# Reciprocals of the softmax sums by way of DRAM rows instead of a spread, a transpose and a copy

## Chip, cores and metric

One core of one Trainium2 chip. The metric is the device time of one execution in microseconds, the median of the runs. Engines are named as in the profile: PE is TensorE, DVE is VectorE, ACT is ScalarE, POOL is GpSimd, SP is the engine that here only issues DMAs.

## What is computed

One layer of a diffusion transformer trunk in float32: adaLN-modulated norms around a mixing layer (pooling in one half of the width, 2-D neighbourhood attention in the other) and a squared-ReLU MLP. SEQ = 1024 latent tokens on a grid of 16 rows by 64 columns, 256 context tokens, 8 heads of 64. The change touches the attention alone:

```python
s_loc = jnp.einsum('bnqhd,brnkhd->bhnqrk', q_r, k_b).astype(jnp.float32) * scale
...
s_loc = jnp.where(col_mask, s_loc + bias.astype(jnp.float32), -jnp.inf)
s_ctx = jnp.einsum('bnqhd,bkhd->bhnqk', q_r, k_ctx).astype(jnp.float32) * scale
...
s = jnp.concatenate([s_loc.reshape(B, H, NA_NCB, NA_QB, n_loc), s_ctx], axis=-1)
p = jax.nn.softmax(s, axis=-1).astype(v.dtype)
...
o = (jnp.einsum('bhnqrk,brnkhd->bnqhd', p_loc, v_b)
     + jnp.einsum('bhnqk,bkhd->bnqhd', p_ctx, v_ctx))
```

## The kernel before

The attention is cut into 32 units. Unit i has a pair of heads, `j = i // 8` (e = 0, 1 in the code), and a band of 8 grid columns, `m = i % 8`, which is 128 queries. Its keys are the bands m-1, m, m+1 (128 each) and the 256 context tokens: 640, or 512 in the bands at the edges (m = 0 and 7), which here are called edge units.

Queries stand on partitions in the scores and in the probabilities. For the product with the values, keys have to stand on partitions, so PE turns the probabilities by transposes in 64-row halves. The result of the value products, `pa`, has the head's channels on partitions and the 128 queries along the free axis. The softmax is divided only there: by then the reciprocal of each query's sum is needed in another layout, constant over the 64 partitions of a head and running over queries along the free axis.

One Python loop of N + 4 = 36 passes writes the work out, shifted: in pass i, `weighed(i - 4)`, then `scores(i)` (PE, then DVE adds bias and mask with a running minimum, `nm`, line 998), `turn(i - 2)` and `fifth_kept(i - 2)`, the exponentials `exps(i, ...)` on ACT, `turn_kept(i - 2, ...)`, `share(i - 1)` and `values(i - 3)`. The order on PE, ACT, DVE and SP is the order of the loop (`in_order`); each engine waits by semaphores only.

The names that matter:

- `share` (1009): DVE takes the reciprocal `ri` (128 x 2) of the two sums, and spreads it to `rb`, 128 x 128 (`tensor_copy`, 1013).
- `turn` (1018): PE transposes, first the two halves of `rb`, then in inner units the fifth block of the probabilities, into `sides`, which are columns of the PSUM banks `pa` and `pz`; then the other blocks into the banks `T` (1026).
- `fifth_kept` (1036): ACT copies the sides to SBUF, `px` (1040): 192 columns each in inner units, 64 in edge units.
- `turn_kept` (1042): ACT and DVE copy the two `T` banks to `pt`.
- `values` (1048): PE adds the value products up in `pa` (1060), 128 of its columns for even units and 128 for odd ones.
- `weighed` (1065): DVE multiplies `pa` by the turned share in `px` and writes the heads' page `f` (1070).

The units' loop also holds the loads of the output weights and their splitting. On SP's queue stand, in the order of the loop: the table loads `U` (876) in passes 2, 10 and 18; `accsh` in pass 4; `ss` in passes 5 and 6; `wor` (1102) in passes 8, 16, 26 and 28; `Ga` in pass 30; six loads `to1`, `bo22`, `to3` of the output weights (1143) in pass 32, 512 KB each. POOL builds the bias tables (883) and issues accumulating DMAs (188), among them two in pass 32 that add a second weight block to `to1`. From pass 32 on the first output products (`pox`) run on PE between the last units: x[0] in pass 32 to x[3] in pass 35. After the loop, PE goes on with `pox`, `poz` and `poy`, then with the MLP.

Of the kernel before, what the change touches and what calls it, by code (L numbers as in the profile page):

```python
# [11 lines left out]
F32 = mybir.dt.float32  # L12
# [6 lines left out]
P = 128  # L19
# [7 lines left out]
HD = 64  # L27
# [8 lines left out]
NM = GW // QC  # L36
# [44 lines left out]
def hybrid_block(ctx, tc, x, ctx_in, w_mod, b_mod, gp1, gp2, w_in, pool_w, rpb, w_out, w1, w2, vectors,  # L81
                 mask, edge, out):
    nc = tc.nc
    sub, mul, add = ALU.subtract, ALU.mult, ALU.add
# [6 lines left out]
    dram = ctx.enter_context(tc.tile_pool(name="dram", bufs=1, space=DRAM))  # L91
# [4 lines left out]
    def sm(name, n, bufs=1):  # L96
        return small.tile([P, n], F32, tag=name.split("_")[0], name=name, bufs=bufs)
# [173 lines left out]
    with tc.tile_pool(name="ps1", bufs=6, space=PSUM) as ps1, tc.tile_pool(name="tmp1", bufs=3) as tmp:  # L271
# [53 lines left out]
        inverse = {}  # L325
# [235 lines left out]
        for k in range(KT):  # L561
            for i in range(2):
                o = (k % 2) * 256 + i * P
# [235 lines left out]
        def row_sum(i):  # L799
            name, _, k = rows[i]  # L800
            if name not in accs:
# [5 lines left out]
        turns = {"w": iter([(pair_load, pair_split, i) for i in range(len(pairs))]),  # L807
                 "r": iter([(row_load, row_sum, i) for i in range(len(rows))])}
# [122 lines left out]
        with in_order(ET.PE, ET.Pool, ET.Activation, ET.DVE, ET.SP) as pooling:  # L931
            banks = {of: [bank(f"p{of}{j}") for j in range(2)] for of in "KQ"}
            use(-1)
            for step, (n, of, j) in enumerate([(n, of, j) for n, of in products for j in range(2)]):
                half_product(n, of, j, banks[of])
                use(step)
                if step in (5, 9, 17):
                    name = {5: "S1", 9: "S4", 17: "S3"}[step]
# [4 lines left out]
                if step in (7, 11):  # L943
                    name = {7: "S4", 11: "S3"}[step]
# [11 lines left out]
    with (  # L956
# [52 lines left out]
        def share(i):  # L1009
            ri = sm(f"ri_{i}", 2, 2)  # L1010
            nc.vector.reciprocal(ri, sums[i])
            shares[i] = att.tile([P, P], F32, tag="ri", name=f"rb{i}", bufs=2)
            nc.vector.tensor_copy(shares[i].rearrange("p (e t) -> p e t", e=2),
                                  ri.rearrange("p (e o) -> p e o", o=1).to_broadcast([P, 2, HD]))

        def turn(i):
            inner = 0 < units[i][1] < NM - 1
            t = [bank(f"T{i}_{h}") for h in range(2)]  # L1020
            turned[i] = t
            halves = [slice(h * HD, (h + 1) * HD) for h in range(2)]

            def both(to, src):
                for h, hs in enumerate(halves):
                    nc.tensor.transpose(to(h), src(hs), ident[hs, hs])  # L1026

            both(lambda h: sides[h][:, :HD], lambda hs: shares[i][hs])
            for e in range(2 if inner else 0):
                both(lambda h: sides[h][:, (e + 1) * HD : (e + 2) * HD], lambda hs: probs[i, e][hs, 4 * P : 5 * P])  # L1030
            for c in range(4):
                for e in range(2):
                    o = (4 * e + c) * HD
                    both(lambda h: t[h][:, o : o + HD], lambda hs: probs[i, e][hs, c * P : (c + 1) * P])

        def fifth_kept(i):
            n = (3 if 0 < units[i][1] < NM - 1 else 1) * HD
            fifths[i] = att.tile([P, 384], F32, tag="px", name=f"px{i}", bufs=4).rearrange("p (h t) -> p h t", h=2)
            for h in range(2):
                nc.scalar.copy(fifths[i][:, h, :n], sides[h][:, :n])  # L1040

        def turn_kept(i, h, copy):
            if h == 0:
# [4 lines left out]
        def values(i):  # L1048
            j, m = units[i]
            vc = [vcp[:, 0:512], vcp[:, 512:1024]]  # L1050
            if 0 < m < NM - 1:
                vs = vb[m - 1 : m + 2] + vc
            else:
                o = 1 if m == 0 else 0
                vs = vc + vb[m + o - 1 : m + o + 1]
            cols = slice((i % 2) * P, (i % 2 + 1) * P)
            for c, v in enumerate(vs):
                for e in range(2):
                    f = (2 * j + e) * HD
                    nc.tensor.matmul(pa[e * HD : (e + 1) * HD, cols], v[:, f : f + HD],  # L1060
                                     turns[i][:, e, c] if c < 4 else fifths[i][:, :, (e + 1) * HD : (e + 2) * HD],
                                     start=(c == 0), stop=(c == len(vs) - 1))


        def weighed(i):
            j, m = units[i]
            if m == 0:
                heads[j] = page(f"f{j}")
            to = heads[j].rearrange("p (m h t) -> p m h t", h=2, t=HD)[:, m, ::-1, ::-1]
            nc.vector.tensor_tensor(to, pa[:, (i % 2) * P : (i % 2 + 1) * P].rearrange("p (h t) -> p h t", h=2),  # L1070
                                    fifths[i][:, :, :HD], mul)

        N = len(units)

# [61 lines left out]
        both = [page(f"ss{i}") for i in range(2)]  # L1136
# [15 lines left out]
        with in_order(ET.PE, ET.Activation, ET.DVE, ET.SP) as projected:  # L1152

            def last_query(n, j):
                half_product(n, "Q", j, last_queries)
                kept_product(n, "Q", j, last_queries[j])
# [3 lines left out]
            for i in range(N + 4):  # L1160
# [49 lines left out]
                else:  # L1210

                    t = i - N
# [51 lines left out]
    with tc.tile_pool(name="ps2", bufs=6, space=PSUM) as ps2:  # L1264
# [6 lines left out]
      with ExitStack() as tmp2:  # L1271
# [58 lines left out]
        with tc.issue_after(projected[ET.DVE]), tc.issue_after(projected[ET.Activation]), in_order(ET.Activation, ET.DVE) as added:  # L1330
# [21 lines left out]
            c = {}  # L1352
# [484 lines left out]
        with tc.issue_after(first[ET.PE]), in_order(ET.PE, ET.Activation, ET.DVE, ET.SP):  # L1837
# [153 lines left out]
```

## Time and profile before

| | |
|---|---|
| median of 3 runs | 1033.1 us (1032.53 to 1033.29) |
| span of the profiled execution, first to last instruction | 1030.8 us |
| mean granted TensorE clock in it | 0.998 |
| PE, DVE, ACT, POOL busy | 1017.8, 751.8, 543.7, 110.7 us |
| first scores of unit 0 | 218.8 us |
| first output product of pass 32 | 322.3 us |

The profile is of one execution; its times are counted from the first instruction. A row of a group reads: line, engine, operation, output<-input, shapes, count | busy time in all, mean ns of one | idle time of the engine just before them, with what ended it. A timeline row reads: start, duration, engine, line, operation. A row of the chain of waits reads: start, duration, what it was. A DMA issue reads: tensors, queue, count, KB each, median us from issue to landing.

### The profile page before, as it was taken

How to read it: one execution, taken by the hardware profiler on the slowest of the kernel's cores; microseconds unless marked ns; L12 is line 12 of the kernel's file. 1: busy time of each engine (PE TensorE's matmuls, PEld its weight loads, DVE VectorE, ACT ScalarE, POOL GpSimd, SP SyncE). 2: the span in 40 equal slices, each digit the busy share in tenths (PEclk: the TensorE clock that was granted, in tenths of full speed). 3: DMA queues.
4: the chain of work that ended last, by engine and by line, in shares of the span. 5: the costliest groups of instructions: out<-in, count | busy, mean ns of one | idle time of the engine just before them, and what ended most of it. 6: DMA issues, size and time to landing. Idle time of an engine off the chain costs nothing.

```text
span 1030.8 us, 15588 instructions
## 1 busy us (share of the span) xinstructions
PE 1017.8 (99%) x5782; PEld 834.2 (81%) x5782; DVE 751.8 (73%) x1187; ACT 543.7 (53%) x941; POOL 110.7 (11%) x168
## 2 busy tenths in 40 slices
PE   8999999999999999999999999999999999999997
PEld 6788888877887888888888888888888888888885
DVE  5588767858996587878998887855766666547576
ACT  7573255328887556776655544555543334334431
POOL 3011200244311311310000000000000000000001
PEclk9999999999999999999999999999999999999999
DMA  9999798632337866795786666637967766555556
GB/s 343 332 255 338 246 265 296 204 86 80 72 95 194 203 180 200 253 237 168 267 269 210 204 210 214 205 122 241 327 220 271 248 226 220 202 180 189 176 182 211
DMA packets 123132, 222.68 MB, mean 216 GB/s; under 512 B 9456, under 2 KB 55152, under 8 KB 123056
## 3 DMA queue, kind: packets, MB, share of 16 engines
q1 hardware_dynamic: 96560, 171.14, 50.4%
q0 software_dynamic: 9360, 19.58, 9.5%
q10 hardware_dynamic: 17136, 30.97, 8.0%
q8 instruction: 45, 0.74, 0.3%
q14 instruction: 31, 0.25, 0.1%
HBM read 168.16 MB, written 52.45 MB: 214 GB/s over the span
## 4 chain that ended last, share of the span: by engine, by line
PE 95%; DMA 2%; ACT 1%; DVE 1%; issue 0%; SPq 0%; DVEq 0%; POOLq 0%; ACTq 0%
PE pu L449 4%; PE S L984 4%; PE pa L1060 3%; PE phv L198 3%; PE phz L198 3%; PE phx L198 3%; PE pyx L198 3%; PE phx L200 3%; PE phv L199 3%; PE phx L199 3%; PE pyx L199 3%; PE pyx L200 3%; PE pyv L199 3%; PE pyv L198 3%; PE pyz L199 3%; PE pyz L198 3%
## 5 line engine op out<-in xcount | busy, mean ns | idle before, releaser
L1007 ACT ACTIVATE sp<-sp,nm 128x640 f32<-128x640 f32 (+1 forms) x64 | 51.4, 803 | 20.0 <-DVE nm L998 19.6
L1577 ACT ACTIVATE c<-c 128x512 f32<-128x512 f32 x48 | 30.3, 632 | 47.0 <-DVE c L1697 28.2
L146 ACT CAST wpS<-S 128x512 fp32r<-128x512 f32 x64 | 38.7, 616 | 26.4 <-PE phv L200 9.2
L198 PE MATMUL phx<-thB,wpA 128*128 128x512 f32 x128 | 50.2, 392 | 0.0
L200 PE MATMUL phx<-thB,wpA 128*128 128x512 f32 x128 | 49.8, 389 | 0.0
L199 PE MATMUL phx<-tlB,wpA 128*128 128x512 f32 x128 | 49.8, 389 | 0.0
L152 DVE TENSOR_TENSOR wpS<-S,wpS 128x512 fp32r<-128x512 f32 x64 | 43.4, 685 | 8.3 <-ACT wpS L146 8.3
L998 DVE CUSTOM_DVE_ANT_0 sp<-S,tab 128x640 f32<-128x640 f32 (+1 forms) x56 | 42.9, 803 | 8.8 <-PE S L984 7.3
L1578 ACT ACTIVATE c<-c 128x512 f32<-128x512 f32 x48 | 30.3, 631 | 15.1 <-DVE sa L1660 12.3
L140 POOL TENSOR_TENSOR ry<-vy,nhalf 128x1 f32<-128x1 f32 x8 | 5.9, 740 | 280.7 <-DVE vy L138 280.7
L198 PEld LDWEIGHTS phx<-thB,wpA 128*128 128x128 f32 x128 | 24.0, 188 | 5.5 <-ACT s L1628 0.5
L984 PE MATMUL S<-kT,q 64*128 64x384 f32 (+1 forms) x128 | 27.9, 495 | 0.3 <-DVE nm L998 0.3
L200 PEld LDWEIGHTS phx<-thB,wpA 128*128 128x128 f32 x128 | 24.0, 188 | 5.0
L199 PEld LDWEIGHTS phx<-tlB,wpA 128*128 128x128 f32 x128 | 24.0, 188 | 4.9
L1060 PE MATMUL pa<-pt,v 128*64 128x128 f32 x352 | 25.9, 279 | 0.6 <-ACT px L1040 0.2
L1045 DVE COPY pt<-T 128x512 f32<-128x512 f32 x32 | 22.0, 686 | 5.5 <-PE T L1026 5.5
L198 PE MATMUL phv<-thT,wpA 128*128 128x512 f32 x64 | 25.1, 392 | 0.0
L198 PE MATMUL phz<-thB,wpS 128*128 128x512 f32 x64 | 25.0, 391 | 0.0
L200 PE MATMUL phv<-thT,wpA 128*128 128x512 f32 x64 | 24.9, 389 | 0.0
L199 PE MATMUL phv<-tlT,wpA 128*128 128x512 f32 x64 | 24.9, 389 | 0.0
L200 PE MATMUL phz<-thB,wpS 128*128 128x512 f32 x64 | 24.9, 389 | 0.0
L199 PE MATMUL phz<-tlB,wpS 128*128 128x512 f32 x64 | 24.9, 389 | 0.0
(1100 smaller groups left out, 3359.7 us busy)
## 6 DMA issues: line engine op xcount, KB each, us to landing
b<-in_w SPq DMA_DIRECT2D x64, 512.0 KB, 4.2
hrS<-hdS SPq DMA_DIRECT2D x32, 512.0 KB, 5.1
hrA<-hdA SPq DMA_DIRECT2D x24, 512.0 KB, 5.5
wm<-in_w_mod SPq DMA_DIRECT2D x16, 512.0 KB, 9.7
wa_0w<-in_w SPq DMA_DIRECT2D x16, 512.0 KB, 5.3
wa_1w<-in_w SPq DMA_DIRECT2D x16, 512.0 KB, 4.5
hdA<-c ACTq DMA_DIRECT2D x32, 256.0 KB, 2.8
hdS<-sa ACTq DMA_DIRECT2D x32, 256.0 KB, 2.7
```

The source lines that it names most:

```text
L146: nc.scalar.copy(hi, src)
L152: nc.vector.tensor_tensor(lo, src, hi.bitcast(F32), sub)
L198: nc.tensor.matmul(ps, ahi, bhi, start=first, stop=False, skip_group_check=more)
L199: nc.tensor.matmul(ps, ahi, blo, start=False, stop=False, skip_group_check=more)
L200: nc.tensor.matmul(ps, alo, bhi, start=False, stop=last, skip_group_check=more)
L449: nc.tensor.matmul(pus[b][j], wk(wgt, k, low, j * P, P), r, start=(k == 0 and n == 0), stop=(k == KT - 1 and n == 2))
L984: nc.tensor.matmul(S[e][:, c0 : c0 + keys.shape[1]], q[hs, cols], keys[hs], start=True, stop=True)
L998: nc.vector.tensor_tensor_reduce(out=to, in0=s, in1=bt, scale=1.0, scalar=BIG, op0=add, op1=ALU.min, accum_out=nm)
L1007: nc.scalar.activation(sp, sp, AF.Exp, bias=least[i, e], scale=-1.0, accum_out=sums[i][:, e : e + 1])
L1060: nc.tensor.matmul(pa[e * HD : (e + 1) * HD, cols], v[:, f : f + HD], turns[i][:, e, c] if c < 4 else fifths[i][:, :, (e + 1) * HD : (e + ...
L1577: nc.scalar.activation(r, src, AF.Relu)
L1578: nc.scalar.activation(r, r, AF.Square)
```

## The change

`share` keeps the reciprocal and stores it, transposed, as two rows of 128 numbers in a DRAM tile `inv` (six of them in turn). A new function `spread` loads each row back repeated over the 64 partitions of its head, which gives `rb` at once in the layout of `pa`; it stands in pass i + 2, ahead of the next unit's `share`. `weighed` reads `rb`. The spreading copy and the two transposes of `rb` go; `px` holds the fifth block alone, and edge units copy nothing there.

```diff
-        sides = (pa[:, 256:448], pz[:, :192])
+        sides = (pa[:, 256:384], pz[:, :128])
+        inverse = {}
...
         def share(i):
             ri = sm(f"ri_{i}", 2, 2)
             nc.vector.reciprocal(ri, sums[i])
-            shares[i] = att.tile([P, P], F32, tag="ri", name=f"rb{i}", bufs=2)
-            nc.vector.tensor_copy(shares[i].rearrange("p (e t) -> p e t", e=2),
-                                  ri.rearrange("p (e o) -> p e o", o=1).to_broadcast([P, 2, HD]))
+            inverse[i] = dram.tile([2, P], F32, tag=f"inv{i % 6}", name=f"inv{i}")
+            nc.sync.dma_start(inverse[i].rearrange("e t -> t e"), ri)
+
+        def spread(i):
+            shares[i] = att.tile([P, P], F32, tag="ri", name=f"rb{i}", bufs=4)
+            for e in range(2):
+                nc.sync.dma_start(shares[i][e * HD : (e + 1) * HD], inverse[i][e : e + 1, :].to_broadcast([HD, P]))
...
-            both(lambda h: sides[h][:, :HD], lambda hs: shares[i][hs])
             for e in range(2 if inner else 0):
-                both(lambda h: sides[h][:, (e + 1) * HD : (e + 2) * HD], lambda hs: probs[i, e][hs, 4 * P : 5 * P])
+                both(lambda h: sides[h][:, e * HD : (e + 1) * HD], lambda hs: probs[i, e][hs, 4 * P : 5 * P])
...
         def fifth_kept(i):
-            n = (3 if 0 < units[i][1] < NM - 1 else 1) * HD
-            fifths[i] = att.tile([P, 384], F32, tag="px", name=f"px{i}", bufs=4).rearrange("p (h t) -> p h t", h=2)
+            if not 0 < units[i][1] < NM - 1:
+                return
+            fifths[i] = att.tile([P, 256], F32, tag="px", name=f"px{i}", bufs=4).rearrange("p (h t) -> p h t", h=2)
             for h in range(2):
-                nc.scalar.copy(fifths[i][:, h, :n], sides[h][:, :n])
+                nc.scalar.copy(fifths[i][:, h], sides[h])
...
-                                    fifths[i][:, :, :HD], mul)
+                                    shares[i].rearrange("p (h t) -> p h t", h=2), mul)
...
+                if 1 < i <= N + 1:
+                    spread(i - 2)
                 if 0 < i <= N:
                     share(i - 1)
```

In the kernel after the change the lines of `values`, `weighed` and the loads of pass 32 are 1065, 1075 and 1148.

More of the change, by code (lines that the diff above doesn't have):

```diff
@@ L1060, in values @@
                     nc.tensor.matmul(pa[e * HD : (e + 1) * HD, cols], v[:, f : f + HD],
-                                     turns[i][:, e, c] if c < 4 else fifths[i][:, :, (e + 1) * HD : (e + 2) * HD],
+                                     turns[i][:, e, c] if c < 4 else fifths[i][:, :, e * HD : (e + 1) * HD],
                                      start=(c == 0), stop=(c == len(vs) - 1))
```

## The prediction

> **What bounds the kernel now.** I read the page first, then the chain of waits inside the attention, then the PE timeline of one pass, then groups and DMA views for the prices.
>
> ```profile
> span 1030.8 us, 15588 instructions
> PE 1017.8 (99%) x5782; PEld 834.2 (81%) x5782; DVE 751.8 (73%) x1187; ACT 543.7 (53%) x941; POOL 110.7 (11%) x168
> ```
>
> TensorE is busy for nearly the whole span. The attention is one loop of 36 passes: 32 that begin one unit each, and four more in which the first output products run between the last units. The chain of waits through pass 29, in order of time:
>
> ```profile
> 312.95 1.28 PE S L984 x8
> 314.23 0.05 PE pa L1026
> 314.28 0.01 PE pz L1026
> 314.28 0.06 PE pa L1026
> ...
> 314.41 0.50 PE T L1026 x16
> 314.90 1.24 PE pa L1060 x20
> 316.15 1.28 PE S L984 x8
> ```
>
> One pass is 3.20 us, and PE's pieces fill it without a gap: scores 1.28, turning through `pa`/`pz` 0.18, turning through `T` 0.50, values 1.24. So a piece taken out of PE's row shortens the pass, as long as no other engine becomes late. VectorE is not late: its largest group in the attention mostly waits for PE.
>
> ```profile
> L998 DVE CUSTOM_DVE_ANT_0 sp<-S,tab 128x640 f32<-128x640 f32 (+1 forms) x56 | 42.9, 803 | 8.8 <-PE S L984 7.3
> ```
>
> **What is removed.** Per unit: two PE transposes of the spread reciprocals, one VectorE copy, and the share's 64 columns of two ScalarE copies.
>
> ```profile
> L1026 PE MATMUL pa<-ident,rb 64*128 64x64 f32 x32 | 7.4, 232 | 0.0
> L1026 PE MATMUL pz<-ident,rb 64*128 64x64 f32 x32 | 7.3, 228 | 0.0
> L1013 DVE COPY rb<-ri 128x128 f32<-128x128 f32 x32 | 7.5, 236 | 1.1
> L1040 ACT COPY px<-pa 128x192 f32<-128x192 f32 x24 | 7.6, 318 | 4.3 <-PE pz L1026 3.9
> L1040 ACT COPY px<-pa 128x64 f32<-128x64 f32 x7 | 1.5, 212 | 3.4 <-PE pz L1026 3.3
> ```
>
> The first two rows add up to 14.7 us of busy time, but that isn't what they cost, since matmuls overlap:
>
> ```profile
> 314.06 0.22 PE L1026 MATMUL pa<-ident,rb 64*128 64x64 f32 x1
> 314.07 0.22 PE L1026 MATMUL pz<-ident,rb 64*128 64x64 f32 x1
> 314.12 0.22 PE L1026 MATMUL pa<-ident,sp 64*128 64x64 f32 x1
> ```
>
> The `rb` pair starts at 314.06 and the next pair at 314.12: a pair occupies 0.06 us of PE's row, as in the chain (0.05 + 0.01). 32 units by 0.06 is **-1.9 us**. The VectorE copy (236 ns) lies in VectorE's idle time and counts nothing. The ScalarE copy of `pa` shrinks from 192 to 128 columns, between 318 and 212 ns, so by some 0.053 us; the value products wait for it. Between nothing and 32 x 0.053 = 1.7 I take **-0.4**, nearer to nothing, because in the chain above PE follows PE and not ScalarE.
>
> **What is added on SP's queue.** Per unit a store of 256 single numbers (`inv`), issued when VectorE's reciprocal is done (end of pass i+1), and two loads of 64 x 512 B (`rb`), issued in pass i+2 when the store has landed. No such store is in the trace. Nearest rows: small loads on SP's queue (32 KB each),
>
> ```profile
> L243 SPq DMA_DIRECT2D gpa<-in_gp x4: 347/416/698, 201.9 to 203.5; - x4
> ...
> DMA to landing us min/median/max: 1.8/2.0/2.1
> ```
>
> and on Pool's queue one-row stores to DRAM (`gsc`) and a load of 1024 single numbers (`sc`):
>
> ```profile
> gsc<-accsc POOLq DMA_DIRECT2D x4, 1.0 KB, 1.6
> sc<-gsc POOLq DMA_DIRECT2D x1, 4.0 KB, 3.0
> ```
>
> Four `gpa` loads go out in 1.6 us from first to last, so one issue takes 0.53. I take a load as 2.0. The store lies between 1.6 and 3.0; with a quarter of the pieces of `sc` I take 1.6 + 1.4/4 = 1.95. From reciprocal to landed row: 1.95, 0.53 for the second issue, 2.0, together 4.5 us. What is available:
>
> ```profile
> 291.47 0.15 DVE L1011 RECIPROCAL ri<-su 128x2 f32<-128x2 f32 x1
> 297.96 0.28 DVE L1070 TENSOR_TENSOR f<-pa,px 128x128 f32<-128x128 f32 x1
> ```
>
> These are the reciprocal of unit 20 and, two passes on, its weighing. From the end of the one (291.62) to the start of the other lie 6.34 us, or 6.15 without the copy of 0.19 that stands ahead of the weighing. The slack is 1.6 us: in a quiet pass the row is in time. SP's own cycle is the store's 1.95, about 0.05 to wake, and two issues, 1.06: 3.06 us. The mean pass, from the chain of waits, 22 passes apart:
>
> ```profile
> 250.42 1.28 PE S L984 x8
> ...
> 319.35 1.06 PE S L984 x8
> ```
>
> 68.93 / 22 = 3.13 us. SP just keeps up, so a delay is made up hardly at all, until VectorE has waited for it.
>
> When the row is late, VectorE waits in `weighed`. Behind it in VectorE's order stand the next unit's masked scores, so ScalarE's exponentials and PE's scores wait as well; and PE's next writes into `pa` wait for that weighing. A late row is a late PE.
>
> Rows can be late where a large transfer stands ahead of them on the queue: passes 4, 5, 6, 8, 10, 16, 18, 26, 28 and 30 have one, and until now SP ran them ahead of their passes, as nothing held it.
>
> ```profile
> L1102 SPq DMA_DIRECT2D wor<-in_w_out x4: 374/380/396, 236.7 to 295.7; - x4
> ...
> DMA to landing us min/median/max: 3.5/3.7/5.5
> ```
>
> 512 KB need 3.7 us where a small load needs 2.0, 1.7 longer: about the slack, 0.1 late each. The slowest needed 5.5, 3.5 longer and 1.9 late; that would meet about three passes in which Pool's accumulating DMAs run. So 0 to 6 us in all; I take **+1.5**: ten passes at 0.15, since most transfers took the median.
>
> **The end of the attention.** Six loads of 512 KB (`to1`, `bo22`, `to3`) belong to pass 32. Before, SP issued them ahead:
>
> ```profile
> 308.06 0.37 SPq L1143 DMA_DIRECT2D to_0w<-in_w_out  x1
> ...
> 319.21 0.37 SPq L1143 DMA_DIRECT2D to_3w<-in_w_out  x1
> ```
>
> Now they stand behind the store of unit 30, which needs the reciprocal in the first row below; and the loads of unit 30's own row stand behind them. Its weighing is the second row, and in the program as built the value products of unit 31 (third row) wait for that weighing.
>
> ```profile
> 322.27 0.15 DVE L1011 RECIPROCAL ri<-su 128x2 f32<-128x2 f32 x1
> ...
> 333.01 0.28 DVE L1070 TENSOR_TENSOR f<-pa,px 128x128 f32<-128x128 f32 x1
> ```
> ```profile
> 335.50 0.66 PE L1060 MATMUL pa<-pt,vc 128*64 128x128 f32 x8
> ```
>
> So six loads start at about 323.5 instead of over 308 to 319. Pool's two accumulations into `to1` wait for the first two of them and run into the rest. What they did to the queue before, from 308 to 322:
>
> ```profile
> q1 hardware_dynamic: 1345, 2.60, 56.0%
> ...
> to_0w<-in_w_out POOLq DMA_DIRECT2D x1, 512.0 KB, 11.4
> to_1w<-in_w_out POOLq DMA_DIRECT2D x1, 512.0 KB, 13.1
> to_3w<-in_w_out SPq DMA_DIRECT2D x1, 512.0 KB, 10.2
> ```
>
> SP's queue moved 2.60 MB in the 13.9 us from its first load, 187 GB/s, 2.8 us for 512 KB; alone it is 1.7 us (3.7 less 2.0). Two loads alone and four in company are 3.4 + 11.2 = 14.6 us, to 338.1. The row of unit 30 lands some 0.5 later, the weighing and the handover take another 0.5: values of unit 31 at 339.1 instead of 335.5, **+3.6 us** of an idle PE. Bounds: all six alone, 10.2 us, to 333.7, nothing; all six in company, 16.8 us, +5.3. I take 3.6, since the accumulations can't start before the first load has landed. What comes after, weights and sums of the output products, is gated by PE's own progress there and shifts with it.
>
> That a small load comes late behind large ones on one queue is in the trace:
>
> ```profile
> L509 SPq DMA_DIRECT2D edg<-in_edge x1: 497/497/497, 53.3 to 53.3; - x1
> DMA to landing us min/median/max: 5.5/5.5/5.5
> ```
>
> 5.5 us, against 2.0 for `gpa`, right behind weight loads. The Trainium skill (DMA: Bandwidth & Descriptors, section on queues, rings and completion order) says that each DMA engine consumes one queue's descriptors in ring order, and takes turns only between queues: by that the row of unit 30 can't pass the six loads. The trace agrees with it in this row. By that rule the sum below holds; if the row could overtake, its +3.6 would be zero and the sum -0.8.
>
> **Sum.** -1.9 - 0.4 + 1.5 + 3.6 = **+2.8 us**. The profiled execution's span of 1030.8 would become 1033.6. The runs' median is 1033.1, 2.3 over the span, for what lies around it; I carry that over: **1035.9 us**. Other parts cost nothing: `tables` of the next head pair get their loads some 8 us later, but are first used six passes (19 us) later.
>
> **Rivals.**
> *All hidden, the PE time is won.* If the six loads take the lower bound (333.7) and large transfers stay within the slack, only -2.3 is left: 1030.8. For: the slack of 1.6. Against: `to_3w` took 10.2 us beside the accumulations.
> *Half and half.* The end costs about half, 1.8, and the passes 0.5: no change, 1033.1.
> *SP sets the pace.* If the store takes more than 2.0 us, SP's cycle exceeds the pass, and the stage runs at SP's rate. At 2.5: 3.61 against 3.13, 0.48 by 28 units is 13.4, less the slack of 1.6, plus the end's 3.6, less the 2.3 won only in part: about +13, 1046. For: `sc` with its single numbers took 3.0. Against: `gsc`, a store to DRAM, took 1.6. The Trainium skill (DMA: Bandwidth & Descriptors, Specifications) says that pieces under 512 B are written by read-modify-write, which speaks for this one; it gives no time, and no row here shows one.
> *Durations add up.* If the transposes cost their busy time, 14.7 us, less the end: about -10, 1023. Against it stand their starts, 0.06 apart.
>
> **Chances.** Forecast 0.50, all hidden 0.16, half and half 0.11, SP's pace 0.20, durations 0.03. The forecast's own range: end 0 to 5.3 and passes 0 to 6, seldom both at an end: 1033 to 1040. To hold 8 in 10 the range takes in the hidden case at 1030.8 (with the 1.7 of the copies in part: 1030.3) and SP's pace up to 1047; the rest is left out. About 2 us, 0.2%, is what a measurement can tell from no change. Of the forecast's 0.50 some 0.08 lies within it and 0.01 below. Slower: 0.41 + 0.20 = 0.61; same: 0.08 + 0.11 = 0.19; faster: 0.01 + 0.16 + 0.03 = 0.20.
>
> **What would show it.** Right: passes of plain units at about 3.14 us instead of 3.20; VectorE idle before `f` (L1075) for a DMA of `rb` in a few passes only; SP issuing `to_0w` at about 320 to 323; PE idle 2 to 5 us before the values of unit 31, released by `f`. Wrong: stores landing in 2.5 us or more and VectorE waiting for `rb` in nearly every pass (SP's pace); no PE idle time before those last values (hidden); or passes still at 3.20, if PE's piece was not what set them.

## The result, and the profile after

| | before | after |
|---|---|---|
| median of 4 runs each | 1033.1 us (1032.53 to 1033.29) | 1242.6 us (1240.43 to 1243.2) |
| after / before | | 1.2025, 95% interval 1.201 to 1.2039 |
| span of the profiled execution | 1030.8 us | 1240.2 us |

The change costs 209 us. The forecast was +2.8 us, with a range that ended at 1047. The first lines of the page of the kernel after:

```profile
span 1240.2 us, 15602 instructions
PE 1078.2 (87%) x5718; PEld 875.9 (71%) x5718; DVE 748.3 (60%) x1155; ACT 538.1 (43%) x925; POOL 110.3 (9%) x168
PEclk9999999876666666869999999999999999999999
```

The damage lies in one stretch, the slices in which the granted clock stands at 6 to 8. By windows (start:end, length, busy time of PE, PEld (its weight loads), DVE, ACT and POOL with their instructions, clock, DMA share, GB/s), two of the kernel after and then one of the kernel before, its last 680 us as the second is of the kernel after:

```profile
300.00:400.00 100.00, 51.88 (x464) 39.03 (x462) 27.08 (x73) 27.53 (x73) 14.00 (x29) 0.67 0.47 33
560.00:1240.00 680.00, 672.91 (x3002) 556.14 (x3000) 495.32 (x639) 338.71 (x516) 36.22 (x48) 1.00 0.66 216
```
```profile
350.60:1030.60 680.00, 672.88 (x3000) 555.43 (x2998) 494.99 (x639) 338.66 (x516) 37.67 (x50) 1.00 0.67 217
```

In the attention PE is busy for half of the time. In the 680 us behind it PE is busy for the same time as before, 672.9 us. The new store and the new loads (name, count, duration of the issue, first and last start, and time to landing), and who waited for them:

```profile
L1014 SPq DMA_DIRECT2D inv<-ri x32: 367/537/898, 228.3 to 525.5; - x32
DMA to landing us min/median/max: 7.3/8.3/16.8
...
L1019 SPq DMA_DIRECT2D rb<-inv x64: 444/540/985, 238.6 to 542.8; - x64
DMA to landing us min/median/max: 2.5/3.4/12.4
```
```profile
DVE f L1075 <- DMA rb<-inv: 145.2, 31, 17.2
...
PE pa L1031 <- DVE f L1075: 112.5, 23, 10.8
```

These last rows read: who waited for whom, us in total, times, longest. The store lands after 8.3 us; 1.95 had been put into the sum. VectorE waits for the row in 31 of 32 passes, and PE waits for VectorE. The chain of waits inside one stretch shows who sets the pace:

```profile
266.93 8.22 DMA inv<-ri
...
275.17 0.47 SPq L1019
275.69 0.59 SPq L1019
...
276.38 8.35 DMA inv<-ri
```

Store, two issues of the loads, next store: SP goes round once in 9.45 us. From the first to the last store it is 525.5 - 228.3 = 297.2 us, 9.59 a pass. In the kernel before, the 32 reciprocals, which the stores now follow, took 326.9 - 227.8 = 99.1 us:

```profile
L1011 DVE RECIPROCAL ri<-su x32: 153/155/157, 227.8 to 326.9; 128x2 f32<-128x2 f32 x32
```

198 of the 209 us lie there, and 11 at the end. There the loads of unit 30's row stand behind the six large loads and land 12.4 us after their issue, the longest in the rows above, and PE stands still for 15.77 us before the values of unit 31:

```profile
537.72 1.12 PE L1065 MATMUL pa<-pt,vc 128*64 128x128 f32 x8 [15.77 <-DVE f L1075]
```

What does a store of 1 KB do for 8 us? First the packets of SP's queue (q1) from 276.4 to 278.4, behind the issue at 276.38 (packets, MB, share of 16 engines); then the time until the landing as a window:

```profile
q1 hardware_dynamic: 432, 0.07, 71.5%
```
```profile
278.50:284.60 6.10, 5.52 (x48) 4.39 (x50) 2.20 (x6) 2.33 (x7) 0.00 (x0) 0.50 0.03 3
```

Of the 432 packets 128 are the 512 B rows of the two loads that went out just ahead of the store, and 304 have 4 B, the store's 256 pieces among them. Then for 6 us the DMA engines do almost nothing (a share of 0.03, one packet, which is not of SP's queue). The pieces have left the engines, and the store still has not landed. This pointed to the memory behind them, and to the first question of the experiments.

### The profile page after: what moved, and what is told of

Its sections match the earlier page's. It is cut to its first block, busy times and chain, and to the rows that moved or that the text cites. A ratio compares the mean times of both kernels' runs of the same rounds, so it can differ in the third digit from the quotient of the medians.

```text
span 1240.2 us, 15602 instructions
## 1 busy us (share of the span) xinstructions
PE 1078.2 (87%) x5718; PEld 875.9 (71%) x5718; DVE 748.3 (60%) x1155; ACT 538.1 (43%) x925; POOL 110.3 (9%) x168
## 4 chain that ended last, share of the span: by engine, by line
PE 72%; DMA 23%; SPq 3%; DVE 1%; issue 1%; ACT 0%; DVEq 0%; POOLq 0%; ACTq 0%
DMA inv<-ri 20%; PE pu L449 4%; PE phz L198 2%; PE phv L198 2%; PE phx L198 2%; PE pyx L198 2%; PE phx L200 2%; PE pyv L200 2%; PE pyx L200 2%; PE pyz L200 2%; PE pyz L199 2%; PE pyv L199 2%; PE phv L199 2%; PE phz L199 2%; PE phx L199 2%; SPq L1019 2%
## 5 line engine op out<-in xcount | busy, mean ns | idle before, releaser
L1031 PE MATMUL pa<-ident,sp 64*128 64x64 f32 x48 | 11.2, 328 | 112.5 <-DVE f L1075 112.5
L1075 DVE TENSOR_TENSOR f<-pa,rb 128x128 f32<-128x128 f32 x32 | 9.3, 292 | 146.8 <-DMA rb<-inv 145.2
L1031 PEld LDWEIGHTS pa<-ident,sp 64*128 64x128 f32 x48 | 6.8, 192 | 123.6 <-DVE f L1075 123.6
L1065 PE MATMUL pa<-pt,vc 128*64 128x128 f32 x160 | 22.3, 395 | 29.4 <-DVE f L1075 29.4
L1065 PE MATMUL pa<-pt,v 128*64 128x128 f32 x352 | 42.3, 403 | 3.8 <-DVE f L1075 3.7
L985 PE MATMUL S<-kT,q 64*128 64x384 f32 (+1 forms) x128 | 39.4, 688 | 0.4 <-DVE nm L999 0.4
L1065 PEld LDWEIGHTS pa<-pt,vc 128*64 128x64 f32 x160 | 15.2, 208 | 30.7 <-issue 16.2
L1065 PEld LDWEIGHTS pa<-pt,v 128*64 128x64 f32 x352 | 31.8, 207 | 6.5 <-DVE f L1075 4.0
L1031 PE MATMUL T<-ident,sp 64*128 64x64 f32 x512 | 31.3, 287 | 0.0
L1031 PEld LDWEIGHTS T<-ident,sp 64*128 64x128 f32 x512 | 29.0, 199 | 1.1 <-issue 0.5
```

Source lines behind the costliest of these rows:

```text
L985: nc.tensor.matmul(S[e][:, c0 : c0 + keys.shape[1]], q[hs, cols], keys[hs], start=True, stop=True)
```

## The experiments

Times are compared with runs of the kernel before on the same chip, 1032.6 to 1033.0 us. Where no ratio stands, the time is of one execution.

### What the store costs, and where

**Two pieces instead of 256.**

```diff
-            ri = sm(f"ri_{i}", 2, 2)
-            nc.vector.reciprocal(ri, sums[i])
+            ri = flat[i % 2]                     # 128 x 128
+            nc.vector.reciprocal(ri[:, :2], sums[i])
...
-            nc.sync.dma_start(inverse[i].rearrange("e t -> t e"), ri)
+            nc.sync.dma_start(inverse[i], ri[0:2, :])
```

> The store of each unit keeps its place on SP's queue, its wait for the reciprocal and its 1 KB, but goes out as two pieces of 512 B (two partitions of the tile that the reciprocal writes into) instead of 256 pieces of 4 B; the factors that come back are not the reciprocals. Theory A (the number or smallness of the pieces makes the store land after 8.3 us, and SP, which waits for the landing, sets the pace of 9.4 us a pass): the store lands in 1.6 to 2.0 us, SP's cycle is 2.7 to 3.1 us, passes are back at 3.13 us, and what is left is the rest of the forecast's sum, some 1033 to 1040 us in all. Rival B (any store to DRAM that is read back at once takes 8 us here, whatever its pieces): the landing stays near 8 us and the time near 1240 us. Rival C (the landing of the loads, 3.4 us, or the two issues of 0.53, hold the pass too): the store lands in 2 us, and passes still stand at 4 to 6 us, 1060 to 1120 us.

1040.9 us, ratio 1.0082 (1.0068 to 1.0095). SP's timeline:

```profile
316.55 0.38 SPq L1015 DMA_DIRECT2D inv<-row  x1
318.02 1.09 SPq L1020 DMA_DIRECT2D rb<-inv  x2
319.21 0.42 SPq L1015 DMA_DIRECT2D inv<-row  x1
```

The loads, which wait for the store, start 1.47 us after its issue. SP's cycle is 2.66 us, under the pass. Same bytes, same queue, same waits: 202 of the 209 us are gone, so they belonged to the pieces. What is left, 8 us, is taken up further down.

**128 pieces of 8 B.**

```diff
-            nc.sync.dma_start(inverse[i].rearrange("e t -> t e"), ri)
+            nc.sync.dma_start(inverse[i].rearrange("e t -> (e t)").rearrange("(t e) -> t e", e=2), ri)
```

> The store writes the 128 x 2 reciprocals as they lie, 128 pieces of 8 B side by side in DRAM, instead of 256 pieces of 4 B in two rows (the factors that come back are in a wrong order). Same bytes, half the pieces. Theory A (landing grows with the number of pieces; 2.0 us fixed and 6.3 us for 256): it lands in about 5.2 us, SP's cycle is about 6.3 us, and the kernel takes some 1240 - 31 x 3.1 = 1145 us. Rival (a fixed cost of any store with pieces below a line, whatever their number): 8.3 us, 1240 us. Rival (the transposing order of the pieces, two far writes per partition, is what costs): near 2 us, 1035 us.

```profile
DMA to landing us min/median/max: 3.2/4.6/11.9
```

1128.5 us, and 4.6 us to landing where 5.2 were expected: with half the pieces the cost is less than half, some 20 ns for each beyond a fixed 2 us (2.6 / 128; with 256 pieces 6.3 / 256 = 25; the 2 us are an estimate from the small loads). The order of the pieces changed with their number, so this run alone does not separate the two.

**The pieces far apart, and in SBUF.** First 512 B apart, then 64 B apart (`n` = 128 and 16), then into two rows in SBUF:

```diff
+        wide = [dram.tile([2 * P, n], F32, tag=f"wide{k}", name=f"wide{k}") for k in range(6)]
...
-            nc.sync.dma_start(inverse[i].rearrange("e t -> t e"), ri)
+            nc.sync.dma_start(inverse[i].rearrange("(e t) s -> t e s", e=2)[:, :, 0], ri)
```

> The 256 pieces of 4 B are written 512 B apart in DRAM instead of side by side (the loads still read 512 B in a row, so the factors that come back are mostly the fill). In the trace of the change the DMA engines are through with the pieces 2 us after the issue and nearly idle (busy share 0.03) for the 6 us until the landing; so the pieces wait in the memory. Theory A1 (each small write takes its turn there, about 25 ns, wherever it goes): landing stays at about 8 us, 1235 to 1245 us in all. Rival A2 (neighbouring pieces share a stretch of memory that has to be read, changed and written back for each, one after the other): apart they overlap, landing falls to 2 to 3 us, SP's cycle to 3.1 to 4.1 us, and the kernel takes 1040 to 1070 us.

> As the run with pieces 512 B apart, which landed in 2.8 us (median), but the 256 pieces of 4 B are written 64 B apart. It asks how large the stretch of memory is within which pieces wait for each other. Theory A3 (a line of 64 B or less): as with 512 B, landing about 2.8 us and 1070 us in all. Rival A4 (a stretch of 512 B, so that 8 pieces still share one, where side by side 128 share it): landing between, 3.2 to 6 us, 1080 to 1170 us. Rival A5 (the distance only spreads the pieces over more memory banks, gradually): close to A4 and not told apart from it by this run.

```diff
-            inverse[i] = dram.tile([2, P], F32, tag=f"inv{i % 6}", name=f"inv{i}")
-            nc.sync.dma_start(inverse[i].rearrange("e t -> t e"), ri)
+            inverse[i] = att.tile([2, P], F32, tag="inv", name=f"inv{i}", bufs=2)
+            for e in range(2):
+                nc.sync.dma_start(inverse[i][e : e + 1, :], ri[:, e : e + 1])
```

> The same 256 pieces of 4 B are written into two rows in SBUF instead of DRAM (as two stores of 128 pieces, one per head), and each load brings a row to one partition of a constant tile only, so the factors are wrong. Theory A (the wait is in DRAM): both stores land about 2 us after the issue; SP's cycle is two stores' issues 1.1, landing 1.5 to 2, two loads' issues 1.1, so 3.7 to 4.2 us, and the kernel takes 1050 to 1070 us. Rival (256 descriptors or packets of 4 B take 8 us wherever they go): landing 6 to 8 us, 1200 us or more.

The stores' landing in the three runs, in the order 512 B, 64 B, SBUF:

```profile
DMA to landing us min/median/max: 1.6/2.8/12.4
```
```profile
DMA to landing us min/median/max: 1.7/2.9/12.4
```
```profile
DMA to landing us min/median/max: 1.9/2.2/11.2
```

1070.6, 1069.6 and 1070.3 us. The 256 pieces of 4 B need 8.3 us side by side in DRAM and 2.8 and 2.9 apart; in SBUF each of the two stores of 128 pieces needs 2.2. So it is neither the number of pieces alone nor their size: small neighbours in DRAM wait for each other.

How long the stretch is within which they wait is not settled. The Trainium skill (DMA: Bandwidth & Descriptors, Specifications) says that pieces below 512 B are written by read-modify-write. A reading and writing back of each shared stretch, one after the other, would look like this. An estimate from the landings: if the 128 pieces that lie side by side in 512 B took turns, each would take 6.3 / 128 = 0.05 us, and 64 B apart, with eight in such a stretch, the store would land 7 x 0.05 = 0.34 us later than with 512 B between them. It landed 0.1 us later, in the median and in the minimum. By the same working a stretch of 128 B would add 0.2 and one of 64 B nothing. So the stretch is more likely 64 or 128 B than 512, but another reason why near pieces wait is not excluded. The chip's way of doing it was not seen, only its times.

All three still took 37 us more than before: with over 2 us for the store and 1.1 for two issues SP's cycle is above the pass of 3.13. In the run with 512 B the loads of one unit start at 256.78 us and those of the third unit after it at 268.44, 3.89 us a pass.

**Stores issued by ScalarE.** So that SP waits for no landing before the next store:

```diff
-            ri = sm(f"ri_{i}", 2, 2)
+            ri = sm(f"ri_{i}", 2, 6)
...
-            nc.sync.dma_start(inverse[i].rearrange("e t -> t e"), ri)
+            nc.scalar.dma_start(inverse[i].rearrange("e t -> t e"), ri)
```

> The stores are issued by ScalarE instead of SP, and the reciprocals have six buffers instead of two, so that the next store does not wait for the landing of the one before; the loads stay on SP, and each still waits for its store. Nothing else changes. Theory C1 (the 8.3 us are latency, stores can overlap, and the pace came from SP's wait for the landing before the next store): a store every pass; from reciprocal to landed row 8.3 + 0.6 + 3.4 = 12.3 us, then about 2.5 us from that weighing to the reciprocal three units on, so 14.8 us for three passes, 4.9 us a pass, and some 1035 + 30 x 1.8 = 1090 us. Rival C2 (the pieces occupy the DMA engines or the memory for those 8 us, so that stores follow each other at 8 us each whoever issues them): landing grows beyond 8.3 us, passes stay at 8 us or more, 1200 us or more. Rival C3 (the latency alone is decisive only once, since PE has other work): 1045 us or less.

The four executions took 1179.8 to 1209.0 us; the ratio 1.1507 (1.1432 to 1.1583) is that of the two shorter ones, and the profile is of the shortest. None of the three theories had it. All issues of the store, the landing of the loads (known for 11 of 64), and the first three stores with the loads behind them:

```profile
L1014 ACTq DMA_DIRECT2D inv<-ri x32: 366/366/413, 227.8 to 457.8; - x32
...
DMA to landing us min/median/max: 5.8/9.2/13.6
```
```profile
227.75 0.38 ACTq L1014 DMA_DIRECT2D inv<-ri  x1
230.51 0.37 ACTq L1014 DMA_DIRECT2D inv<-ri  x1
233.11 0.37 ACTq L1014 DMA_DIRECT2D inv<-ri  x1
...
237.64 2.41 SPq L1019 DMA_DIRECT2D rb<-inv  x4
...
246.97 4.03 SPq L1019 DMA_DIRECT2D rb<-inv  x2
```

Stores can overlap: the loads of the first two units go out one behind the other from 237.64 on, so both stores had landed by 239 or so, the second 8.4 us after its issue at most. So C2, 8 us for each store in turn, does not hold in this form. But stores can also stretch: SP waited for the third until 13.9 us after its issue, and over all 32 the median from a store to its first load is 9.4 us. And the loads take 9.2 us instead of 3.4: they are now issued while the next unit's store is under way. From reciprocal to row it is 9.4 + 0.5 + 9.2 = 19.1 us, and with the 2.5 to the reciprocal three units on 21.6 / 3 = 7.2 us a pass, where the stores went out every (457.8 - 227.8) / 31 = 7.4 us. C1's way of reckoning held, with the landings in it too short, that of the loads above all. That the loads wait for the neighbours' writes is an inference from these landings; no run here separates it from other causes.

### What the transposes were worth

```diff
-            inverse[i] = dram.tile([2, P], F32, tag=f"inv{i % 6}", name=f"inv{i}")
-            nc.sync.dma_start(inverse[i].rearrange("e t -> t e"), ri)
...
-            shares[i] = att.tile([P, P], F32, tag="ri", name=f"rb{i}", bufs=4)
-            for e in range(2):
-                nc.sync.dma_start(shares[i][e * HD : (e + 1) * HD], inverse[i][e : e + 1, :].to_broadcast([HD, P]))
+            shares[i] = flat[1]                  # a constant tile
```

> No store and no loads: the reciprocal is computed, and the weighing multiplies by a constant tile instead. What is left of the change is what it takes away: the two transposes of the spread reciprocals per unit, the spreading copy, and a third of a ScalarE copy. By the prediction's steps: -1.9 us from PE's row and -0.4 from the ScalarE copy, 1030.8 us against 1033.1. Rival (a transpose costs its busy time, 14.7 us in all): 1018 to 1022 us. Rival (PE's pieces do not set the pass, or the time is won in the passes and lost at the end of the attention): 1033 us.

1030.1 us against 1032.6, ratio 0.9977 (0.9968 to 0.9986): -2.5 us, forecast -2.3. The transposes cost their starts and not their busy time. More than this no form of the change that keeps a store and two loads can be expected to win.

### With a cheap store: the rest of the sum

In the two-piece run PE has five gaps in the passes (1.01, 0.39, 0.28, 1.24 and 0.31 us, 3.2 in all; the largest is shown; the one of 0.28 ends with ScalarE's copy `px`, the others with `f`), and the end shows the forecast's wait. The window behind it shows something that was not in the forecast:

```profile
301.00 0.27 PE L1032 MATMUL pa<-ident,sp 64*128 64x64 f32 x1 [1.24 <-DVE f L1076]
...
341.58 0.66 PE L1066 MATMUL pa<-pt,vc 128*64 128x128 f32 x8 [3.76 <-DVE f L1076]
```
```profile
342.00:346.00 4.00, 4.00 (x22) 3.10 (x18) 2.12 (x5) 0.00 (x0) 1.78 (x2) 0.62 0.18 30
```

PE stands for 3.76 us before the values of unit 31, and in the 4 us after that its clock is 0.62.

**The six loads behind the last row.** The block of pass 32 that issues `to1`, `bo22` and `to3` is moved behind `spread` of pass 33; the two-piece store stays.

```diff
-                if i == N:
-                    t1 = [out_load(f"to1_{kk}w", kk, 1) for kk in (0, 1)]
...
                 if 1 < i <= N + 1:
                     spread(i - 2)
+                if i == N + 1:
+                    t1 = [out_load(f"to1_{kk}w", kk, 1) for kk in (0, 1)]
```

> The kernel with the two-piece store (factors not the reciprocals), and the six loads of pass 32 with their two accumulations moved behind the loads of the last row, on the same queue. Nothing else. Theory D (the prediction's end term: row 30 waits on SP's queue behind the six loads; PE idle for 3.76 us before the values of unit 31 in the two-piece run, and a lower clock after it): that stall goes or shrinks below 1 us, and the time falls from 1040.9 by 4 to 6.5 us, to 1034.5 to 1037. Rival (the loads are then late for the output products, and the wait moves there): 1039 us or more, with PE idle after 345 us. Rival (the stall is due to the last units' own chain, not to the loads): 1040.9 unchanged.

```profile
317.42 0.27 PE L1032 MATMUL pa<-ident,sp 64*128 64x64 f32 x1 [1.38 <-DVE f L1076]
...
364.44 0.76 PE L198 MATMUL poz<-to_0h,S 128*128 128x512 f32 x1 [4.80 <-DVE ns L1401]
```
```profile
363.60 0.69 DVE L1132 TENSOR_TENSOR mp<-pox,Ga 128x512 f32<-128x512 f32 x1 [1.88 <-DMA to_3w<-to_1w]
```

1042.5 us, ratio 1.0097 (1.0082 to 1.0112). The gap before the values of unit 31 is gone, so it did come from the six loads; but now the weights come late: VectorE, for which PE stands 4.80 us at 364, had itself just waited for Pool's accumulation `to_3w<-to_1w`. The first rival was right: the six loads have a deadline on both sides.

**A cheap store with the full function.** VectorE turns 32 x 32 blocks, and the store writes 8 pieces of 128 B; in the second run the four `wor` and the six loads of pass 32 go to ScalarE's queue (`nc.scalar.dma_start` in their two lines).

```diff
+            ri, rt = flat[i % 2], flip[i % 2]    # 128 x 64 each
+            nc.vector.reciprocal(ri.rearrange("p (e x) -> p e x", e=2)[:, :, 0], sums[i])
+            nc.vector.transpose(rt, ri)
...
+            nc.sync.dma_start(inverse[i].rearrange("e (b q) -> b e q", q=32), rt[::32].rearrange("b (e q) -> b e q", e=2))
```

> The same function as the change, in fewer pieces: VectorE turns 32 x 32 blocks, so that the two rows lie on four partitions, and the store writes 8 pieces of 128 B. Theory A (pieces cost, and 8 are few): the store lands in about 1.5 to 2.0 us, SP keeps up, and the time is that of the two-piece run, 1040.9 us, within 1.5. Rival (a piece below 512 B costs a fixed extra, so 128 B are no better than 4 B): landing 4 us or more, 1080 us or more.

> As the kernel with turned blocks, and the four loads wor and the six loads of pass 32 are issued by ScalarE, at the same places of the loop, so that they stand on another queue than the rows. Theory D (the row of unit 30 waits in its queue behind the six loads, and single rows behind wor; in the two-piece run PE was idle for 3.76 us before the values of unit 31 and its clock fell to 0.96 in that stretch): the end's stall goes, and with it 3.8 us and most of the 3 us that the lower clock cost; 1032 to 1035 us, against 1040.9 with the loads ahead. Rival (the row shares the DMA engines with the six loads whichever queue they are on): it lands as late as before, 1038 to 1042 us.

1048.8 us (ratio 1.0154, 1.014 to 1.0168) and 1052.1 us (1.0184, 1.017 to 1.0198); both expectations missed. In the first the gaps were larger than with two pieces, at the end 6.07 us. In the second ScalarE, which now issues the six loads, waited itself:

```profile
350.26 1.12 PE L1067 MATMUL pa<-pt,vc 128*64 128x128 f32 x8 [6.07 <-DVE f L1077]
```
```profile
343.77 0.62 ACT L1089 CAST mix<-f 128x512 fp32r<-128x512 f32 x1 [6.65 <-DMA bo_2w<-in_w_out]
```

Moving the loads to a working engine moved the wait to that engine. By the pages the first run's span is 9.7 us longer than that of the two-piece run (1047.5 and 1037.8): PE is idle for 5.1 us more, and busy for 4.6 us more with the same 5718 matmuls (1022.4 and 1017.8). Why its rows are late more often stays open; the turning, 0.25 us of VectorE a unit, and a longer issue of the store, 0.57 instead of 0.38 us, are part of it at most.

**One pass more for each row.** As the first of these two, with the six loads behind the last row, and `weighed(i - 5)` instead of `weighed(i - 4)`; `pa` holds three stretches of values in turn (columns 0, 128, 384).

> The full function: blocks turned on VectorE, 8 pieces of 128 B per store, the six loads of pass 32 behind the last row, and each unit weighed one pass later (three stretches of the bank pa in turn instead of two), so that a row has about 9.3 us instead of 6.2. Theory E (with the store cheap, what was left against the run without DMA, 1030.1 us, were rows just too late for their pass and the order at the end): no PE idle time for rows in the passes, 1031 to 1034 us, so about the time before or 0.2 per cent under it. Rival (SP's own cycle, store, wait and two loads, about 3.1 to 3.6 us, sets the pace, and slack does not help): PE idles as in the run with turned blocks, 1040 to 1046 us. Rival (the later weighing costs at the end of the attention, where PE has no other unit to work on): 1036 to 1040 us.

1045.9 us, ratio 1.0129 (1.0112 to 1.0146). That is in the range of the rival, SP's own cycle, but about half of the loss lies elsewhere: PE's gaps before `f` in the passes are down to 4.3 us in sum, from 7.1 in the first run with turned blocks, and 4.73 us lie at the end, where the six loads behind the last row come late, as in the run before that moved them. So the extra pass helped, as far as one trace of each shows, and the time alone does not tell SP's pace from the late loads. Here the clock can be read by itself. PE had a gap of 1.70 us, released by `f`, and in the 4 us behind it:

```profile
265.54 0.27 PE L1033 MATMUL pa<-ident,sp 64*128 64x64 f32 x1 [1.70 <-DVE f L1077]
...
368.05 0.77 PE L198 MATMUL poz<-to_0h,S 128*128 128x512 f32 x1 [4.73 <-DVE ns L1404]
```
```profile
266.00:270.00 4.00, 4.00 (x40) 3.00 (x36) 3.06 (x9) 3.07 (x8) 3.70 (x6) 0.60 0.26 51
```

40 matmuls in 4 us at a clock of 0.60.

**The store ahead of the loads.** SP's order is turned round, so that a store has a whole pass to land before SP asks for it, the turned row has four buffers instead of two, and the six loads are spread over passes 28 to 33:

```diff
-                if 1 < i <= N + 1:
-                    spread(i - 2)
                 if 0 < i <= N:
                     share(i - 1)
+                if 1 < i <= N + 1:
+                    spread(i - 2)
```

> The full function. From the run with turned blocks and one pass more for each row, three orders are changed: on SP's queue the store of a unit now stands ahead of the loads of the unit before it, so that SP issues a store while the one before has had a pass to land and does not wait for it; the buffers of the turned row are four instead of two; and the six loads of pass 32 are spread, one behind the row in each of passes 28 to 33. Theory F (in that run SP's wait for each landing made it fall behind, which showed as PE gaps of 1.70 and 1.88 us and a clock of about 0.6 for 4 us behind each, and the late loads cost a gap of 4.73 us at 368 us): gaps for rows go below 0.5 us in sum, no fall of the clock in the passes, 1031 to 1034 us, which is between the run without DMA, 1030.1, and a little over the kernel before. Rival (the six loads between the last rows delay these): a gap of 1 to 4 us before the values of unit 31 or 30 and 1035 to 1040 us. Rival (transfers on SP's queue make rows late wherever SP's wait stands): 1040 us or more, with gaps in the passes as before.

```profile
240.00:320.00 80.00, 79.08 (x1178) 63.41 (x1174) 71.52 (x212) 66.88 (x175) 25.28 (x47) 1.00 0.47 114
```
```profile
331.53 0.37 PE L1033 MATMUL pa<-ident,sp 64*128 64x64 f32 x1 [6.03 <-DVE f L1077]
```

1038.3 us, ratio 1.0053 (1.004 to 1.0067). The passes are full (79.08 of 80 us, clock 1.00; in the kernel before 79.59 in the same window), as theory F had it; the end is not, 6.03 us, worse than the first rival's 1 to 4. The order and the buffers were changed together, so their shares are not known.

**Rows for the first 24 units only**, with the reciprocal moved ahead of the pass's scores, and the old transposes for units 24 to 31:

```diff
+                if 0 < i <= FIRST:               # FIRST = 24
+                    share(i - 1)
+                if 1 < i <= N + 1:
+                    spread(i - 2)
                 if i < N:
                     scores(i)
```

> The full function. Units 0 to 23 get their reciprocals by way of DRAM rows (blocks turned on VectorE, 8 pieces of 128 B per store, the store of a unit ahead of the loads of the unit before it; the reciprocal stands ahead of the pass's scores instead of at its end, where VectorE was idle for some 0.16 us before the mask), units 24 to 31 by the spread, transposed and copied shares of the kernel before, and the six loads stay where they were. So SP has no store to wait for from pass 27 on and can run ahead with the six loads as before the change. Theory G (with a cheap store in the right place the rows cost the passes nothing, as the run with the store ahead showed up to 320 us, and what was left were the six loads among the last rows): no PE gap over 0.5 us from 218 to 345 us, the PE time of 24 units is won, 24/32 of 2.4 us, and the kernel takes 1030.5 to 1032 us, 1 to 2 us under the kernel before. Rival (the earlier reciprocal and the turning delay the masked scores, 0.3 us in 24 passes): 1035 to 1040 us. Rival (rows cost the passes something that the last run's gaps don't show): 1033 to 1036 us.

```profile
  ACT sp L1010: 11.7, 18
```
```profile
244.69 0.27 PE L1041 MATMUL pa<-ident,sp 64*128 64x64 f32 x1 [2.43 <-DVE f L1089]
...
251.74 0.70 PE L987 MATMUL S<-kcT,q 64*128 64x256 f32 x4
...
305.74 0.77 PE L987 MATMUL S<-kcT,q 64*128 64x256 f32 x3
```

1038.1 us, ratio 1.005 (1.0036 to 1.0064): the range of the first rival, and its mechanism is there. VectorE waits in 18 passes, 0.65 us each, for the exponentials before it may take the reciprocal, and the masked scores stand behind it. From the scores of unit 8 to those of unit 24 it is 305.74 - 251.74 = 54.0 us, 3.38 a pass; in the kernel before 297.52 - 247.37 = 50.15, 3.13 a pass. But that is 4 us, and as much had been lost by unit 8: one row came late, with a gap of 2.43 us and a clock of 0.65 from 244 to 248. The end has no gap.

**Both halves that had no gap.** Units 0 to 25 as in the run with the store ahead (reciprocal at the end of the pass, weighed after five passes), units 26 to 31 in the old way, and the six loads where they were:

```diff
+        due = lambda i: [u for u in range(N) if u + (5 if u < FIRST else 4) == i]      # FIRST = 26
+        place = lambda i: slice(*((0, P), (P, 2 * P), (3 * P, 4 * P))[i % 3 if i < FIRST else i % 2])
```

> The full function. The two halves of the last two runs put together: units 0 to 25 by rows with the reciprocal at the end of its pass, the store ahead of the loads of the unit before, and one pass more until the weighing (passes without gaps up to 320 us in the run with the store ahead); units 26 to 31 by the old way of transposes, with the six loads where they were (an end without gaps in the run with rows for 24 units, whose passes were 3.51 us because VectorE waited for ScalarE's exponentials before the early reciprocal). Theory G (rows cost the passes nothing with a cheap store in the right place): no PE gap over 0.5 us from 218 to 345 us, 26/32 of the 2.4 us won, 1030.3 to 1031.5 us against 1032.6. Rival (rows cost the passes something that gaps don't show, turning and extra work on VectorE among it): 1032.5 to 1035 us. Rival (the handover from one way to the other at pass 28 to 30 costs a gap and a fall of the clock): 1035 us or more.

```profile
240.00:339.00 99.00, 98.01 (x1373) 79.05 (x1368) 80.80 (x236) 77.45 (x200) 29.84 (x50) 1.00 0.55 139
339.00:350.00 11.00, 11.00 (x51) 9.10 (x50) 7.35 (x10) 6.97 (x15) 4.60 (x5) 1.00 1.04 263
```

1030.75 us (1030.56 to 1031.46) against 1032.8, ratio 0.9981 (0.9972 to 0.999). It beats both kernels: -2.0 us, which is 26/32 of the 2.5. With a cheap store, in the right place and with a pass more, the rows cost the passes nothing.

## Why the prediction was wrong

**The step that failed is the store's price, 1.95 us.** It stood between `gsc` (one row to DRAM, 1.6) and `sc` (1024 single numbers, 3.0). Neither is the new operation. `sc` is a load, its single numbers go to SBUF; the store in SBUF above, 2.2 us, fits that bracket well. 256 neighbouring numbers going to DRAM need 8.3. So the bracket was taken for two bounds when it had no upper end: no row of the trace showed a store of many small pieces to DRAM.

**The margin made it decisive.** The prediction itself reckoned SP's cycle at 3.06 us against a pass of 3.13: with every store over 2.02 us SP sets the pace, and the upper bound had been put at 3.0. Priced at that bound, the formula of that rival gives 4.11 - 3.13 = 0.98 us by 28 units, 27 us, and the same further terms change that by less than 1. The forecast chose a point inside a bracket next to a cliff and gave SP's pace a chance of 0.20.

**The rival's mechanism was right, its size was not.** "SP sets the pace" is what happened: a wait for `rb` in nearly every pass, as its sign had been written down. With 8.3 in its formula, 8.3 + 0.05 + 1.06 = 9.41 us a pass, where 9.59 were measured. It had been priced at 2.5, so at +13, and the range ended there.

**What held.** PE's gain: -2.3 forecast, -2.5 measured with nothing added; its split into transposes and copies was not tested. The end: +3.6 forecast, a gap of 3.76 us in the two-piece run, and gone when the six loads were moved. The row behind large loads on one queue was read rightly. (The upper bound of that term is 5.8 by its own numbers and not 5.3: 323.5 + 16.8 + 1.0 - 335.5.)

**What was too small beside it.** Late rows: 1.5 forecast, gaps of 2.9 us before `f` in the passes of the two-piece run, and 0.3 before a copy. The load was priced too low as well, 2.0 us where the kernel after has 3.4; SP does not wait for it, so it is not in SP's cycle. And a term was missing: the clock that falls behind a gap. The pages of the two-piece run and of the run without DMAs have PE busy for different times with the same matmuls:

```profile
PE 1017.8 (98%) x5718; PEld 834.6 (80%) x5718; DVE 745.5 (72%) x1157; ACT 539.5 (52%) x925; POOL 110.3 (11%) x168
```
```profile
PE 1015.3 (99%) x5718; PEld 834.2 (81%) x5718; DVE 744.7 (72%) x1157; ACT 539.5 (52%) x925; POOL 111.9 (11%) x168
```

That is 2.5 us. Behind the gap of 3.76 us the 4 us at a clock of 0.62 are worth 1.5 of them; where the rest lies stays open. Then -2.5 + 3.2 + 3.8 + 2.5 = +7.0, which is the difference of the profiled spans, 1037.8 and 1030.8. The medians differ by 8.3, since the profiled execution of the two-piece run took 1.3 us less than its median.

## What to carry to other kernels

Do not let a DMA turn a column into a row of DRAM number by number: make the row on chip first, so that the store has few pieces, or it lands microseconds after the DMA engines are through with it. Where the cycle of an in-order queue is within a few per cent of the loop it serves, price the unknown operation at its worst, and put a store ahead of the loads that wait for the store before, so that the queue does not stand at a landing (here this filled the passes together with more buffers and a pass more). A load with a deadline on both sides, like the six here, belongs on a queue that nothing holds.

## What the runs showed of the hardware

- A store of 256 pieces of 4 B landed after 8.3 us with the pieces side by side in DRAM, 2.9 us with a piece every 64 B, 2.8 with one every 512 B; a store of 128 such pieces to SBUF after 2.2; 128 pieces of 8 B side by side after 4.6. The DMA share was 0.03 for the 6 us before the landing.
- Loads of 64 x 512 B that were issued while such a store was under way landed after 9.2 us (11 of 64 known) instead of 3.4.
- A gap of PE of 1.70 us was followed by a clock of 0.60 over the next 4 us, and one of 3.76 us by 0.62; in the passes of the run with the six loads behind the last row, with gaps of up to 1.38 us, it stayed at 1.00 (mean of the stretch behind that gap, first below). The Trainium skill (TensorE: Matmul & The Clock Gate, the table of states in part 1) says that the clock falls after an idle window of about 3.4 us. Here it fell after a gap of half that length. But in the run with the loads on ScalarE's queue a gap of 2.56 us left it at 1.00 (second and third below), so the length of a gap alone does not decide.

```profile
318.00:322.00 4.00, 4.00 (x70) 3.34 (x66) 3.01 (x10) 3.11 (x10) 0.00 (x0) 1.00 0.31 62
```
```profile
256.58 0.88 PE L1067 MATMUL pa<-pt,v 128*64 128x128 f32 x12 [2.56 <-DVE f L1077]
```
```profile
258.00:262.00 4.00, 4.00 (x44) 2.85 (x46) 3.93 (x13) 3.59 (x9) 0.00 (x0) 1.00 0.12 34
```
